# Decoder trunk: VectorE divides the fetched rows, the compressions begin ten k-tiles later with their loads ahead, stored gates get their Silus together, and the paired stages open with steps 0 0 1 1

## The chip, the cores and the metric

One core of a Trainium2 chip runs the kernel. The metric is the device time in microseconds (us). PE is the matmul engine, DVE is VectorE, ACT is ScalarE, POOL is GpSimd, and SP is the engine whose queue issues most DMAs.

## What is computed

One layer of a hybrid decoder: a normalised x (256 tokens, width 4096) goes through one input projection, the result feeds two attention mixers, each mixer's output is normalised and multiplied by a Silu gate, and both go through one output projection onto the residual.

```python
h = _rmsnorm(x, norm_g[l])
proj = h @ w_in[l]
(q_a, k_a, v_a, z_a, q_b, kc, vc, ksl, vsl, kwn, vwn, z_b, g_b) = jnp.split(proj, _split_points(), axis=-1)
o_a = _dilated_mixture(heads(q_a, N_HEADS_A) * (HEAD_DIM ** -0.5), heads(k_a, N_HEADS_A), heads(v_a, N_HEADS_A), slopes_a)
gates = jax.nn.sigmoid(g_b).reshape(B, S, N_HEADS_B, 3)
o_b = _nsa(heads(q_b, N_HEADS_B), kc, vc, ksl, vsl, kwn, vwn, gates, slopes_b, k_pe, k_w1, k_w2, v_pe, v_w1, v_w2)
y_a = _rmsnorm(o_a, out_g_a[l]) * jax.nn.silu(z_a)
y_b = _rmsnorm(o_b, out_g_b[l]) * jax.nn.silu(z_b)
x = x + jnp.concatenate([y_a, y_b], axis=-1) @ w_out[l]
return _rmsnorm(x, final_g)

def _compress(t, pe, w1, w2):       # of kc and of vc
    blocks = t[:, idx] + pe         # 15 blocks of 32 tokens
    return jax.nn.gelu(flat @ w1) @ w2
```

## The kernel before, in words

Every matrix product keeps float32 accuracy by splitting each operand into a high and a low part (`split_to`: ACT copies the high part at L105, DVE subtracts to get the low part at L106) and adding three matmuls (L98, L99, L100). So each block of weights is loaded on SP's queue, split on ACT and DVE, and then multiplied on PE.

The program has five parts. An **opening** (0 to 112 us of the trace) brings in x and computes the columns of kc, vc, kw and the small gates. The **paired input stage** (to about 847 us, `run_pairs`) takes nine pairs of 512-column chunks of w_in, 16 steps each; a fast step saves one of eight products by adding and subtracting blocks first (five DVE instructions, L432 to L439; 21 matmuls), a plain step splits the blocks as they are (one DVE instruction of L106; 24 matmuls). `FIRST` lists for the first pair of a stage which of its steps are fast (1) and plain (0). There are two places for split fast blocks (bf0, bf1) and one for plain blocks (bp). Results leave through POOL-issued DMAs that add into DRAM scratch (`put_sums`, L459). In this stage and its twin the order of the engines is the order of the code.

The **middle stage** (847 to about 1364 us) streams seven chunks of gate columns z (a1 to a3, b0 to b3; 32 k-tiles of six matmuls each) and the first chunk of w_out through PE. Between its k-tiles a list of tasks advances, one piece (up to a `yield`) for each unit of credit; a k-tile gives `pace` units. The tasks are two compressions (`compress`, of kc and of vc, four loads w1 of 1 MB each and 64 matmuls ph of 128x256), four dilated attentions (`attend_a`), `mixer_done` for mixer a, `start_b`, four sparse attentions (`attend_b`), `mixer_done` for b, and last `turn_y`. Here the framework's scheduler sets the order on each engine, and an engine keeps to its order: an instruction that waits holds all behind it. Rows of q, k, sel and qb in scratch were stored before the factor 1/rms (rstd) was put in, so `fetch(..., divide=True)` multiplies them on POOL as soon as they land (L560, two multiplies of 128x512 for each of 13 fetches); PE then transposes them (pt, L592). Values v are multiplied while they are split (L108, L109). `gate_z` takes Silu of each gate chunk as it is finished (L735); a chunk finished before its mixer goes to scratch and comes back later (L712, L720).

Work at the start of this stage: `begin_rest` issues the loads of the constants cmat and of kvc and puts all tasks on the list at once, so the first compression starts with the first k-tile, and its loads of pe, w2 and w1 are issued inside it, one by one.

The **paired output stage** (to about 1610 us) is the twin over w_out, three pairs; it begins with `first_chunk` (residual add, squares and a multiply on the w_out chunk just finished). A **last stage** of plain chunks and the final normalisation ends the program.

Of the kernel before, what the change touches and what calls it, by code (L numbers as in the profile page):

```python
# [11 lines left out]
F32 = mybir.dt.float32  # L12
# [6 lines left out]
P = 128  # L19
SEQ = 256  # L20
NT = SEQ // P
# [23 lines left out]
FIRST = [0, 0, 1, 0, 1, 1, 0, 1, 1, 0, 1, 1, 0, 1, 1, 0]  # L45
# [38 lines left out]
def hybrid_trunk(ctx: ExitStack, tc: tile.TileContext, a: dict):  # L84
# [310 lines left out]
    def run_pairs(w_src, dcs, lhs_of, sops, begin, places, names, out=False):  # L395
# [144 lines left out]

# [86 lines left out]
    def attend_a(hg):  # L627
        vsrc, qsrc = st.pop("va"), st.pop("qa")
        v = split_values(vsrc)
        ksrc = fetch(f"k{hg}", divide=True)  # L630
        yield
        yield from transposed(qsrc, "qa", SCALE)
        yield from transposed(ksrc, "ka")
        if hg < 3:
            st["va"], st["qa"] = fetch(f"v{hg + 1}"), fetch(f"q{hg + 1}", divide=True)
        else:
            st["sel"], st["kw"] = fetch("sel", divide=True), fetch("kw", 2 * HD)
# [66 lines left out]
    waiting, finished, gated = {"a": [], "b": []}, set(), set()  # L704

    def gate(which, i, sz=None):
        r = o_sb["r" + which]
        if sz is None:
            sz = []
            for m in range(NT):  # L710
                sz.append(room["zq"].tile([P, CW], F32, name="sz", tag="zt", bufs=4))
                nc.sync.dma_start(sz[m], scratch(f"z{which}{i}")[:, m])  # L712
            yield
            yield
            if (which, i) == ("a", 0):
                for m in range(NT):
                    nc.scalar.activation(sz[m], sz[m], AF.Silu, scale=rstd[:, m : m + 1])
        for m in range(NT):
            ys = o_at(which, i * CW, CW)[:, m]
            nc.vector.scalar_tensor_tensor(ys, ys, r[:, m : m + 1], sz[m], op0=OP.mult, op1=OP.mult)  # L720
        gated.add((which, i))
        yield

    def mixer_done(which):
        rms_of(which)
        finished.add(which)
        for i in waiting[which]:
            yield from gate(which, i)
        yield

    def gate_z(which, i):
        def done(ps):
            sz = [room["zq"].tile([P, CW], F32, name="sz", tag="zt", bufs=4) for m in range(NT)]
            for m in range(NT):
                nc.scalar.activation(sz[m], ps[m], AF.Silu, scale=rstd[:, m : m + 1])  # L735
            if which in finished:
                tasks.appendleft(gate(which, i, sz))
            else:
                for m in range(NT):
                    nc.sync.dma_start(scratch(f"z{which}{i}")[:, m], sz[m])  # L740
                waiting[which].append(i)
# [46 lines left out]

    def compress(t, which):

        n = "kv"[which]
# [7 lines left out]
        if which == 1:  # L799
            st["va"], st["qa"] = fetch("v0"), fetch("q0", divide=True)  # L800
        pe = room["work"].tile([P, CBL], F32, name="pe", tag="pe", bufs=2)
        nc.sync.dma_start(pe, a[f"cmp_{n}_pe"])
        w2 = room["zq"].tile([P, 2, HD], F32, name="w2", tag="zt", bufs=4)
        w2h = room["work"].tile([P, 2, HD], F32R, name="w2h", tag="pTh", bufs=2)
        w2l = room["work"].tile([P, 2, HD], F32R, name="w2l", tag="pTl", bufs=2)
        nc.sync.dma_start(w2, a[f"cmp_{n}_w2"])
        w1 = {}

        def load_w1(i):
            w1[i] = room["o"].tile([P, 2 * 4, HID], F32, name="w1", tag="o", bufs=4)  # L810
            nc.sync.dma_start(w1[i], a[f"cmp_{n}_w1"][i])

        yield
        bhl = room["o"].tile([P, CBL, 2, 2, NC], F32R, name="bhl", tag="o", bufs=4)
        load_w1(0)
# [9 lines left out]
        load_w1(1)  # L825
# [43 lines left out]
        if which == 0:  # L869
# [5 lines left out]
            nc.vector.memset(kc, 0.0)  # L875
# [19 lines left out]
    def start_b():  # L895
# [20 lines left out]
        put_k(1, kw)  # L916
        yield
# [5 lines left out]
        st["qb"] = fetch("qb0", divide=True)  # L923
# [7 lines left out]
    def attend_b(hg):  # L931
        yield from transposed(st.pop("qb"), "qb", SCALE)
        if hg < 3:
            st["qb"] = fetch(f"qb{hg + 1}", divide=True)
# [11 lines left out]
    def attend_half(hg, m):  # L946
# [36 lines left out]
        def compressed():  # L983
# [13 lines left out]
            nc.vector.memset(c3, 0.0)  # L997
# [101 lines left out]
    def first_chunk(ps, xr, gf):  # L1099

        for m in range(NT):
            r = xr[:, m]
            nc.vector.tensor_add(r, ps[m], r)
# [138 lines left out]
    def begin_rest():  # L1242
# [10 lines left out]
        t = fetch("kvc")  # L1253
# [49 lines left out]
    rest = run_pairs(a["w_out"], dcs, y_lhs, y_sops, begin_out, OUT_PLACES, OUT_BANKS, out=True)  # L1303
# [77 lines left out]
```

## Time and profile before

| | |
|---|---|
| time, median of 3 runs | 1671.77 us (1671.13 to 1672.93) |
| profiled execution, its own time | 1676.31 us |
| its span in the trace | 1674.4 us |
| PE busy | 1621.6 us, 97% of the span |
| DVE busy | 1375.1 us, 82% |
| ACT busy | 1011.5 us, 60% |
| POOL busy | 197.4 us, 12% |
| DMA | 386.71 MB, mean 231 GB/s |

The profiled execution took 4.54 us longer than the median of the runs; 1.91 us of its time lie outside the span. PE is busy nearly always, so what there is to win or lose in this change shows as PE's idle time and as stretches in which PE runs at a lower clock (PEclk: 1.00 is 2.4 GHz, 0.50 is 1.2 GHz).

### The profile page before, as it was taken

How to read it: one execution, taken by the hardware profiler on the slowest of the kernel's cores; microseconds unless marked ns; L12 is line 12 of the kernel's file. 1: busy time of each engine (PE TensorE's matmuls, PEld its weight loads, DVE VectorE, ACT ScalarE, POOL GpSimd, SP SyncE). 2: the span in 40 equal slices, each digit the busy share in tenths (PEclk: the TensorE clock that was granted, in tenths of full speed). 3: DMA queues.
4: the chain of work that ended last, by engine and by line, in shares of the span. 5: the costliest groups of instructions: out<-in, count | busy, mean ns of one | idle time of the engine just before them, and what ended most of it. 6: DMA issues, size and time to landing. Idle time of an engine off the chain costs nothing.

```text
span 1674.4 us, 20936 instructions
## 1 busy us (share of the span) xinstructions
PE 1621.6 (97%) x7743; PEld 1334.6 (80%) x7743; DVE 1375.1 (82%) x1651; ACT 1011.5 (60%) x1259; POOL 197.4 (12%) x224
## 2 busy tenths in 40 slices
PE   8999999999999999999989999899999999999997
PEld 5997778888878888888877777778888878778886
DVE  6769998898889898989857777787866859998984
ACT  6746656565656565656555656676665745656554
POOL 0000111020102020202022211200000000111110
PEclk9999999999999999999999999999999999999999
DMA  9766788887889797979797544443355456798974
GB/s 354 270 229 203 238 265 252 260 256 241 251 246 267 243 282 227 286 231 285 253 318 265 176 142 166 159 164 131 127 200 191 162 202 201 231 274 244 294 282 170
DMA packets 105286, 386.71 MB, mean 231 GB/s; under 512 B 12576, under 2 KB 13216, under 8 KB 93792
## 3 DMA queue, kind: packets, MB, share of 16 engines
q1 hardware_dynamic: 80928, 331.37, 56.3%
q0 software_dynamic: 23824, 52.97, 14.3%
q8 instruction: 60, 0.98, 0.2%
q10 hardware_dynamic: 432, 1.05, 0.2%
q14 instruction: 42, 0.34, 0.1%
HBM read 334.17 MB, written 53.26 MB: 231 GB/s over the span
## 4 chain that ended last, share of the span: by engine, by line
PE 74%; DVE 10%; DMA 6%; issue 5%; ACT 3%; POOL 1%; SPq 0%; ACTq 0%; POOLq 0%; DVEq 0%
PE p L99 14%; PE p L100 13%; PE p L98 13%; PE acc L99 8%; PE acc L100 7%; PE acc L98 7%; DMA bw<-in_w_in 3%; DVE bf L439 2%; PE e L100 2%; PE e L99 2%; PE e L98 2%; DVE bf L438 2%; DVE bt L432 1%; DVE wl L106 1%; DMA w<-in_cmp_v_w 1%
## 5 line engine op out<-in xcount | busy, mean ns | idle before, releaser
L106 DVE TENSOR_TENSOR wl<-w,wh 128x1024 fp32r<-128x1024 f32 (+2 forms) x178 | 209.0, 1176 | 111.1 <-ACT wh L105 110.5
L105 ACT ACTIVATE wh<-w 128x1024 fp32r<-128x1024 f32 (+2 forms) x178 | 180.6, 1018 | 128.4 <-PE acc L100 100.7
L98 PE MATMUL acc<-wh,xh 128*128 128x512 f32 (+2 forms) x640 | 243.3, 382 | 4.0 <-ACT wh L105 4.0
L99 PE MATMUL acc<-wl,xh 128*128 128x512 f32 (+2 forms) x640 | 242.7, 379 | 4.2 <-DVE wl L106 4.1
L439 DVE TENSOR_TENSOR bf<-bt,bf 128x2048 fp32r<-128x2048 f32 x108 | 246.7, 2284 | 0.0
L100 PE MATMUL acc<-wh,xl 128*128 128x512 f32 (+2 forms) x640 | 241.4, 377 | 0.0
L434 ACT ACTIVATE bf<-bt 128x1024 fp32r<-128x1024 f32 x108 | 114.5, 1060 | 187.1 <-DVE bt L432 186.9
L106 DVE TENSOR_TENSOR bp<-bw,bp 128x2048 fp32r<-128x2048 f32 x72 | 164.8, 2288 | 70.1 <-ACT bp L105 70.1
L431 ACT ACTIVATE bf<-bw 128x1536 fp32r<-128x1536 f32 x108 | 160.3, 1484 | 67.2 <-DMA bw<-in_w_in 45.5
L105 ACT ACTIVATE bp<-bw 128x2048 fp32r<-128x2048 f32 x72 | 137.5, 1910 | 88.4 <-PE e L100 69.7
L438 DVE TENSOR_TENSOR bf<-bw,bf 128x1536 fp32r<-128x1536 f32 x108 | 189.1, 1751 | 0.0
L432 DVE TENSOR_TENSOR bt<-bw 128x1024 f32<-128x1024 f32 x108 | 132.0, 1222 | 14.3 <-DMA bw<-in_w_in 11.8
L99 PEld LDWEIGHTS acc<-wl,xh 128*128 128x128 f32 x640 | 122.1, 191 | 23.9 <-DVE wl L106 7.2
L437 ACT ACTIVATE bf<-bt 128x1024 fp32r<-128x1024 f32 x108 | 114.8, 1063 | 42.9 <-DVE bt L436 41.8
L98 PEld LDWEIGHTS acc<-wh,xh 128*128 128x128 f32 x640 | 121.8, 191 | 22.8 <-ACT wh L105 5.5
L100 PEld LDWEIGHTS acc<-wh,xl 128*128 128x128 f32 x640 | 121.7, 190 | 18.7
L99 PE MATMUL p<-bf,sum 128*128 128x512 f32 x324 | 127.7, 394 | 5.3 <-DVE bf L439 5.2
L98 PE MATMUL p<-bf,sum 128*128 128x512 f32 x324 | 126.3, 390 | 0.0
L100 PE MATMUL p<-bf,sum 128*128 128x512 f32 x324 | 126.2, 390 | 0.0
L99 PE MATMUL p<-bp,xh 128*128 128x512 f32 x324 | 126.1, 389 | 0.0
L100 PE MATMUL p<-bp,xl 128*128 128x512 f32 x324 | 126.0, 389 | 0.0
L98 PE MATMUL p<-bp,xh 128*128 128x512 f32 x324 | 126.0, 389 | 0.0
(328 smaller groups left out, 3466.6 us busy)
## 6 DMA issues: line engine op xcount, KB each, us to landing
bw<-in_w_in SPq DMA_DIRECT2D x288, 512.0 KB, 6.3
w<-in_w_in SPq DMA_DIRECT2D x60, 1024.0 KB, 4.9
bw<-in_w_out SPq DMA_DIRECT2D x96, 512.0 KB, 5.0
w<-in_w_out SPq DMA_DIRECT2D x16, 1024.0 KB, 5.4
scr_q<-parts POOLq DMA_DIRECT2D x30, 256.0 KB, 7.9
scr_k<-parts POOLq DMA_DIRECT2D x30, 256.0 KB, 7.9
scr_v<-parts POOLq DMA_DIRECT2D x30, 256.0 KB, 7.8
scr_qb<-parts POOLq DMA_DIRECT2D x30, 256.0 KB, 8.3
```

Source lines behind the costliest of these rows:

```text
L98: nc.tensor.matmul(out, lh, rh, start=start, stop=False)
L99: nc.tensor.matmul(out, lh, rl, start=False, stop=False)
L100: nc.tensor.matmul(out, ll, rh, start=False, stop=stop)
L105: nc.scalar.activation(h, src, AF.Copy)
L106: nc.vector.tensor_sub(l, src, h.bitcast(F32))
L431: nc.scalar.activation(h[:, :3], w[:, B22:], AF.Copy)
L432: nc.vector.tensor_tensor(t[:, T3 : T1 + 1], w[:, B22 : B11 + 1], w[:, B12 : B12 + 1].to_broadcast([P, 2, CW]), op=OP.subtract)
L434: nc.scalar.activation(h[:, 3:5], t[:, T3 : T1 + 1], AF.Copy)
L437: nc.scalar.activation(h[:, 5:], t[:, T2:], AF.Copy)
L438: nc.vector.tensor_sub(l[:, :3], w[:, B22:], h[:, :3].bitcast(F32))
L439: nc.vector.tensor_sub(l[:, 3:], t, h[:, 3:].bitcast(F32))
```

## The change

Five edits go together.

1. `FIRST` is 0 0 1 1 0 1 1 ... in place of 0 0 1 0 1 1 0 ....
2. `fetch` only loads; a new `divide` multiplies by rstd on DVE, called where the rows are about to be transposed, some pieces of the task later. The zeroing of kc and of c3 moves from DVE to POOL.
3. The loads for the compressions are issued at k-tile 3 of the first z chunk (`load_first`) and the compressions start at k-tile 10 (`attentions`); w1 of both compressions is one row of eight loads that runs ahead. `pace` is 1.1 in the first z chunk and 1.5 later (1.45 before).
4. All gate chunks that finish before mixer b is done are stored without their Silu; `mixer_done` loads them two ahead and takes the Silus there. Chunks a3, b0 and b1, which were kept or gated at once before, go through scratch too.
5. In the output stage only the two residual adds stand ahead of the first step; the squares, the multiplies and the store of r0 come after its third step (`store_first`).

```diff
-FIRST = [0, 0, 1, 0, 1, 1, 0, 1, 1, 0, 1, 1, 0, 1, 1, 0]
+FIRST = [0, 0, 1, 1, 0, 1, 1, 0, 1, 1, 0, 1, 1, 0, 1, 0]
...
             split_on(n)
+            if n == 2 and later:
+                later()
...
-    def fetch(key, width=CW, divide=False):
+    def fetch(key, width=CW):
         t = room["zq"].tile([P, NT, width], F32, name="fetched", tag="qk", bufs=2)
         nc.sync.dma_start(t, scratch(key))
-        for m in range(NT if divide else 0):
-            nc.gpsimd.tensor_scalar_mul(t[:, m], t[:, m], rstd[:, m : m + 1])
         return t
+
+    def divide(t):
+
+        for m in range(NT):
+            nc.vector.tensor_scalar_mul(t[:, m], t[:, m], rstd[:, m : m + 1])
...
-        ksrc = fetch(f"k{hg}", divide=True)
+        ksrc = fetch(f"k{hg}")
+        yield
+        divide(qsrc)
         yield
         yield from transposed(qsrc, "qa", SCALE)
+        yield
+        divide(ksrc)
+        yield
         yield from transposed(ksrc, "ka")
...
     def mixer_done(which):
+
         rms_of(which)
         finished.add(which)
-        for i in waiting[which]:
-            yield from gate(which, i)
-        yield
+        loaded = deque()
+        todo = list(waiting)
+        waiting.clear()
...
+        load()
+        if todo:
+            load()
+        for _ in range(3):
+            yield
+        while loaded:
+            z, sz = loaded.popleft()
+            for m in range(NT):
+                nc.scalar.activation(sz[m], sz[m], AF.Silu, scale=rstd[:, m : m + 1] if z == ("a", 0) else 1.0)
+            yield
+            yield from gate(*z, sz)
+            if todo:
+                load()
+            yield
...
+            last = which in finished and "b" in finished
             for m in range(NT):
-                nc.scalar.activation(sz[m], ps[m], AF.Silu, scale=rstd[:, m : m + 1])
-            if which in finished:
+                nc.scalar.activation(sz[m], ps[m], AF.Silu if last else AF.Copy, scale=rstd[:, m : m + 1])
+            if last:
...
+    w1, small = {}, {}
+
+    def load_w1(i):
+
+        if i < 8:
+            w1[i] = room["o"].tile([P, 2 * 4, HID], F32, name="w1", tag="o", bufs=4)
+            nc.sync.dma_start(w1[i], a[f"cmp_{'kv'[i // 4]}_w1"][i % 4])
...
-                split_to(wh, wl, w1[grp // 2][:, hs])
+                split_to(wh, wl, w1[4 * which + grp // 2][:, hs])
                 ready[grp] = (wh, wl)
-                if grp % 2 == 1 and grp // 2 + 2 < 4:
-                    load_w1(grp // 2 + 2)
+                if grp % 2 == 1:
+                    load_w1(4 * which + grp // 2 + 2)
+                if grp == 4 and which == 0:
+                    load_small(1)
...
-            nc.vector.memset(kc, 0.0)
+            nc.gpsimd.memset(kc, 0.0)
...
+    def load_first():
+        st["kvc"] = fetch("kvc")
+        load_small(0)
+        load_w1(0)
+        load_w1(1)
...
-    pace = 1.45
-    waiting["a"].append(0)
+    hooks[0, 3] = load_first
+    hooks[0, 10] = attentions
...
-        add_chunk(w_chunk(c + i), CW, x_lhs, gate_z(which, i), pace=pace)
+        add_chunk(w_chunk(c + i), CW, x_lhs, gate_z(which, i), pace=1.5 if chunks else 1.1)
...
-        first_chunk(first_out, *room["in0"])
+        for m in range(NT):
+            r = room["in0"][0][:, m]
+            nc.vector.tensor_add(r, first_out[m], r)
...
+    def store_first():
+        first_chunk(*room["in0"])
```

SP's queue at the start of the middle stage, in the kernel before. Rows of L811 load w1 (cmp_k of the first compression, cmp_v of the second), L806 loads w2, L254 loads four k-tiles of the z chunk (1 MB; x3 is three such loads in a row), fetched is a fetch from scratch:

```order
L811 DMA w_5836<-in_cmp_k_w 128x2048
L254 DMA w<-in_w_in 128x2048
L806 DMA w_5825<-in_cmp_k_w 128x256
L811 DMA w_5855<-in_cmp_k_w 128x2048
L811 DMA w_5864<-in_cmp_k_w 128x2048
L811 DMA w_5906<-in_cmp_k_w 128x2048
L254 DMA w<-in_w_in 128x2048 x2
L558 DMA fetched<-scr_v_2627 128x1024
```

The same queue now, from behind the first two w1 loads (L820 is the load of w1 now):

```order
L820 DMA w_5842<-in_cmp_k_w 128x2048
L820 DMA w_5844<-in_cmp_k_w 128x2048
L254 DMA w<-in_w_in 128x2048 x3
L824 DMA pe<-in_cmp_v_pe 128x32
L560 DMA fetched<-scr_v_2627 128x1024
L826 DMA w_6011<-in_cmp_v_w 128x256
L254 DMA w<-in_w_in 128x2048
L820 DMA w_5950<-in_cmp_k_w 128x2048
L820 DMA w_5990<-in_cmp_k_w 128x2048
L820 DMA w_6036<-in_cmp_v_w 128x2048
L820 DMA w_6076<-in_cmp_v_w 128x2048
L254 DMA w<-in_w_in 128x2048 x3
```

The third w1 load (w_5950) stood behind one load of z; it stands behind four loads of z and the fetch of v0 now, and the first w1 loads of the second compression have moved up right behind the first compression's.

DVE at the end of the paired input stage and the first rows of the middle stage, before. bp and bf1 are the last split blocks of the paired stage, wl is the low part of two k-tiles of z, w1hl that of half a w1 load:

```order
L106 TENSOR_TENSOR bp_1153<-bw1_1151,bp_1153 128x2048
L106 TENSOR_TENSOR bf1_1154<-bw2_1152,bf1_1154 128x2048
L875 MEMSET kc_6050 128x32
L997 MEMSET c3_7889 128x384
L106 TENSOR_TENSOR wl_5758<-w_5755,wh_5757 128x1024
L106 TENSOR_TENSOR wl_5762<-w_5755,wh_5761 128x1024
L106 TENSOR_TENSOR wl_5768<-w_5765,wh_5767 128x1024
L820 TENSOR_TENSOR bt_5838<-cT_5816,pe_5823 128x480 x2
L106 TENSOR_TENSOR w1hl_5858<-w1_5836,w1hl_5858 128x1024
```

And now, from the last split of the paired stage on:

```order
L106 TENSOR_TENSOR bf1_1154<-bw2_1152,bf1_1154 128x2048
L106 TENSOR_TENSOR wl_5758<-w_5755,wh_5757 128x1024
L106 TENSOR_TENSOR wl_5762<-w_5755,wh_5761 128x1024
L106 TENSOR_TENSOR wl_5768<-w_5765,wh_5767 128x1024
L106 TENSOR_TENSOR w2l_5916<-w2_5840,w2h_5915 128x256
L106 TENSOR_TENSOR wl_5821<-w_5765,wh_5820 128x1024
L106 TENSOR_TENSOR w1hl_5932<-w1_5842,w1hl_5932 128x1024
L106 TENSOR_TENSOR w1hl_5947<-w1_5842,w1hl_5947 128x1024
L106 TENSOR_TENSOR wl_5849<-w_5771,wh_5848 128x1024
L106 TENSOR_TENSOR wl_5865<-w_5771,wh_5864 128x1024
```

The two MEMSETs no longer stand ahead of the first wl, and two splits of the first w1 load have come ahead of the splits of k-tiles 8 and 9 (wl_5849) and later ones.

DVE around the second attention's keys, now. va is the split of the values, qaTl and kaT are the low parts of turned queries and keys, o_a, den and n belong to the attention before:

```order
L669 RECIPROCAL rden_6710<-den_6703 128x2
L109 SCALAR_TENSOR_TENSOR va_6780<-fetched_6549,rstd_71,va_6780 128x4x128
L106 TENSOR_TENSOR wl_6807<-w_6737,wh_6806 128x1024
L106 TENSOR_TENSOR pal_6734<-pt_6729,pah_6733 128x384
L109 SCALAR_TENSOR_TENSOR qaTl_6796<-pt_6797,qaTh_6795 128x512
L109 SCALAR_TENSOR_TENSOR qaTl_6796<-pt_6816,qaTh_6795 128x512
L693 SCALAR_TENSOR_TENSOR o_a0_6553<-po_6755,rden_6710,o_a0_6553 128x128 x2
L566 TENSOR_SCALAR fetched_6785<-fetched_6785,rstd_71 128x512 x2
L106 TENSOR_TENSOR wl_6832<-w_6737,wh_6831 128x1024
L106 TENSOR_TENSOR kaT_6841<-pt_6842,kaT_6841 128x512
L106 TENSOR_TENSOR wl_6888<-w_6804,wh_6887 128x1024
```

The two divides (L566) stand in DVE's row ahead of the splits wl of the z chunk; before, they stood on POOL, with nothing of PE's stream behind them.

## Rows read from the trace of the kernel before

**Rows 1.** Stretches: length, busy PE, PEld, DVE, ACT, POOL; clock, DMA, GB/s.
```profile
840.00:860.00 20.00, 15.91 (x74) 12.63 (x73) 9.46 (x11) 7.93 (x12) 5.30 (x6) 1.00 0.94 297
860.00:890.00 30.00, 28.25 (x154) 22.46 (x151) 20.42 (x27) 16.50 (x22) 4.89 (x6) 1.00 1.06 349
890.00:1100.00 210.00, 190.94 (x989) 152.55 (x990) 159.56 (x380) 137.41 (x251) 43.67 (x25) 0.96 0.47 167
```

**Rows 2.** What PE waited for, 825 to 1370 us: total, times, longest.
```profile
PE pt L592 <- POOL fetched L560: 12.0, 8, 2.7
PE ph L842 <- DVE bhl L106: 5.6, 2, 3.0
PE acc L99 <- DVE wl L106: 2.9, 3, 1.5
PE pt L666 <- DVE n L656: 1.1, 5, 0.3
```

**Rows 3.** Stretches right after PE's waits (columns of rows 1).
```profile
892.30:895.70 3.40, 3.40 (x16) 3.40 (x17) 3.40 (x7) 0.00 (x0) 1.63 (x1) 0.50 1.01 424
...
953.70:957.10 3.40, 3.40 (x12) 2.82 (x10) 1.29 (x2) 2.15 (x5) 0.00 (x0) 0.50 0.51 159
...
1063.80:1069.00 5.20, 5.02 (x17) 4.45 (x18) 2.10 (x4) 1.62 (x3) 2.35 (x3) 0.50 0.51 179
```

**Rows 4.** The tile fetched: multiplies on POOL, ns min/median/max, first and last start.
```profile
L560 POOL TENSOR_SCALAR fetched<-fetched,rstd x26: 1557/1568/3647, 889.4 to 1117.2; 128x512 f32<-128x512 f32 x26
```

**Rows 5.** DVE groups of the last stage: a multiply of the same shape.
```profile
L1161 DVE TENSOR_SCALAR r<-r,rout 128x512 f32<-128x512 f32 x8 | 3.3, 481 | 1.4 <-POOL rout L115 1.4
```

**Rows 6.** The chain that ended last, DMAs in it: start, issue to landing.
```profile
868.46 16.73 DMA w<-in_cmp_v_w
...
945.20 3.75 DMA fetched<-scr_k
...
976.86 6.56 DMA fetched<-scr_k
```

**Rows 7.** SP's DMA queue, 840 to 905 us: packets, MB, share of 16 engines.
```profile
q1 hardware_dynamic: 3181, 17.46, 68.8%
```

**Rows 8.** Timeline, start of the middle stage: start, duration, instruction, idle before.
```profile
847.28 0.39 PE L98 MATMUL acc<-wh,xh 128*128 128x512 f32 x1
...
847.52 0.09 DVE L875 MEMSET kc<- 128x32 f32 x1 [9.23 <-PE e L100]
...
855.64 0.39 PE L98 MATMUL acc<-wh,xh 128*128 128x512 f32 x1
...
856.32 0.39 PE L98 MATMUL acc<-wh,xh 128*128 128x512 f32 x1
859.33 0.33 PE L842 MATMUL ph<-w1hl,bhl 128*60 128x256 f32 x1 [2.61 <-DVE bhl L106]
...
859.61 0.28 PE L842 MATMUL ph<-w1hl,bhl 128*60 128x256 f32 x1
859.72 0.28 PE L843 MATMUL ph<-w1hl,bhl 128*60 128x256 f32 x1
```

**Rows 9.** Timeline of ACT, 926 to 938 us: a Silu and a load of the function table.
```profile
929.53 0.69 ACT L735 ACTIVATE sz<-acc,rstd 128x512 f32<-128x512 f32 x1
930.24 1.28 ACT L655 ACT_TABLE_LOAD   x1
```

**Rows 10.** Timeline of DVE and PE, first pairs of the two paired stages.
```profile
137.48 0.50 PE L99 MATMUL p<-bf,sum 128*128 128x512 f32 x1 [1.24 <-DVE bf L439]
1372.55 1.22 DVE L432 TENSOR_TENSOR bt<-bw 128x1024 f32<-128x1024 f32 x1
1376.94 0.50 PE L99 MATMUL p<-bf,yh 128*128 128x512 f32 x1 [1.49 <-DVE bf L438]
1379.01 2.29 DVE L106 TENSOR_TENSOR bp<-bw,bp 128x2048 fp32r<-128x2048 f32 x1
1379.14 0.50 PE L99 MATMUL p<-bf,ysum 128*128 128x512 f32 x1 [1.24 <-DVE bf L439]
```

More of the change, by code (lines that the diff above doesn't have):

```diff
@@ L393, in hybrid_trunk, with run_pairs @@
     OUT_PLACES, OUT_BANKS = ("f1", "t", "p", "f0", "w"), ("p7", "p1", "p6", "p5", "p4", "p2", "p3", "e")
-    def run_pairs(w_src, dcs, lhs_of, sops, begin, places, names, out=False):
+    def run_pairs(w_src, dcs, lhs_of, sops, begin, places, names, out=False, later=None):
         fast, plain = [[i for i in range(NKP) if FAST[i] == f] for f in (1, 0)]
@@ L629, in attend_a @@
         v = split_values(vsrc)
-        ksrc = fetch(f"k{hg}", divide=True)
+        ksrc = fetch(f"k{hg}")
+        yield
+        divide(qsrc)
         yield
         yield from transposed(qsrc, "qa", SCALE)
+        yield
+        divide(ksrc)
+        yield
         yield from transposed(ksrc, "ka")
         if hg < 3:
-            st["va"], st["qa"] = fetch(f"v{hg + 1}"), fetch(f"q{hg + 1}", divide=True)
+            st["va"], st["qa"] = fetch(f"v{hg + 1}"), fetch(f"q{hg + 1}")
         else:
-            st["sel"], st["kw"] = fetch("sel", divide=True), fetch("kw", 2 * HD)
+            st["sel"], st["kw"] = fetch("sel"), fetch("kw", 2 * HD)
         qh, ql = st["qaT"]
@@ L702, in hybrid_trunk, with gate @@
     yh, yl, turned = [None] * 4, [None] * 4, set()
-    waiting, finished, gated = {"a": [], "b": []}, set(), set()
-    def gate(which, i, sz=None):
+    waiting, finished, gated = [("a", 0)], set(), set()
+    def gate(which, i, sz):
         r = o_sb["r" + which]
[L708 to L712, printed above, removed]
-            yield
[L714 to L717, printed above, removed]
         for m in range(NT):
@@ L726, in mixer_done, with load @@
         finished.add(which)
-        for i in waiting[which]:
-            yield from gate(which, i)
-        yield
+        loaded = deque()
+        todo = list(waiting)
+        waiting.clear()
+        def load():
+            z = todo.pop(0)
+            sz = [room["zq"].tile([P, CW], F32, name="sz", tag="zt", bufs=4) for m in range(NT)]
+            for m in range(NT):
+                nc.sync.dma_start(sz[m], scratch(f"z{z[0]}{z[1]}")[:, m])
+            loaded.append((z, sz))
+        load()
[12 more added lines that the diff above has]
+            yield
     def gate_z(which, i):
@@ L740, in done @@
                     nc.sync.dma_start(scratch(f"z{which}{i}")[:, m], sz[m])
-                waiting[which].append(i)
+                waiting.append((which, i))
         return done
@@ L787, in open_b, with load_small @@
         B["vc3"] = room["work"].tile([3 * Q, 2, HD], F32R, name="vc3", bufs=1)
+    w1, small = {}, {}
[3 more added lines that the diff above has]
+            nc.sync.dma_start(w1[i], a[f"cmp_{'kv'[i // 4]}_w1"][i % 4])
+    def load_small(which):
+        pe = room["work"].tile([P, CBL], F32, name="pe", tag="pe", bufs=2)
+        nc.sync.dma_start(pe, a[f"cmp_{'kv'[which]}_pe"])
+        w2 = room["zq"].tile([P, 2, HD], F32, name="w2", tag="zt", bufs=4)
+        nc.sync.dma_start(w2, a[f"cmp_{'kv'[which]}_w2"])
+        small[which] = pe, w2
     def compress(t, which):
-        n = "kv"[which]
         tT = room["zq"].tile([P, 2, NT, P], F32, name="cT", tag="zt", bufs=4)
@@ L799, in compress @@
         if which == 1:
[L800 to L803, printed above, removed]
+            st["va"], st["qa"] = fetch("v0"), fetch("q0")
+        pe, w2 = small.pop(which)
         w2h = room["work"].tile([P, 2, HD], F32R, name="w2h", tag="pTh", bufs=2)
         w2l = room["work"].tile([P, 2, HD], F32R, name="w2l", tag="pTl", bufs=2)
[L806 to L811, printed above, removed]
         yield
         bhl = room["o"].tile([P, CBL, 2, 2, NC], F32R, name="bhl", tag="o", bufs=4)
-        load_w1(0)
         bt = room["work"].tile([P, CBL, 2, NC], F32, name="bt", tag="qTh", bufs=1)
@@ L824, in compress @@
         yield
-        load_w1(1)
         ph = room["pso"].tile([4 * NC, HID], F32, name="ph", tag="po")
@@ L916, in start_b @@
         put_k(1, kw)
+        divide(sel)
         yield
@@ L922, in start_b @@
         yield
-        st["qb"] = fetch("qb0", divide=True)
+        st["qb"] = fetch("qb0")
         put_v(1, vg[:, :, : 2 * HD])
@@ L931, in attend_b @@
     def attend_b(hg):
-        yield from transposed(st.pop("qb"), "qb", SCALE)
+        for _ in range(0 if hg else 3):
+            yield
+        qb = st.pop("qb")
+        divide(qb)
+        yield
+        yield from transposed(qb, "qb", SCALE)
         if hg < 3:
-            st["qb"] = fetch(f"qb{hg + 1}", divide=True)
+            st["qb"] = fetch(f"qb{hg + 1}")
         first, second = attend_half(hg, 0), attend_half(hg, 1)
@@ L996, in compressed @@
             c3 = live["c"] = room["work"].tile([P, 4, 3, Q], F32, name="c3", tag="c3", bufs=1)
-            nc.vector.memset(c3, 0.0)
+            nc.gpsimd.memset(c3, 0.0)
             for i in range(3):
@@ L1295, in begin_out @@
     def begin_out():
-        first_chunk(first_out, *room["in0"])
+        for m in range(NT):
+            r = room["in0"][0][:, m]
+            nc.vector.tensor_add(r, first_out[m], r)
         psum.close()
         room["banks"] = opened(psum, "banks", 1, space=PS)
+    def store_first():
+        first_chunk(*room["in0"])
         right2.close()
@@ L1302, in hybrid_trunk @@
     ordered.enter_context(tc.manual_schedule())
-    rest = run_pairs(a["w_out"], dcs, y_lhs, y_sops, begin_out, OUT_PLACES, OUT_BANKS, out=True)
+    rest = run_pairs(a["w_out"], dcs, y_lhs, y_sops, begin_out, OUT_PLACES, OUT_BANKS, out=True, later=store_first)
     inner.close()
```

6 lines of the change are left out of this document (3 added, 3 removed).

## The prediction

> **What bounds the kernel now.** PE is busy 97% of the span, so I looked for the stretches where it is not, by stage first. In the middle stage PE loses 4.1 us from 840 to 860, 1.8 us to 890 and 19.1 us to 1100 [rows 1]; and from 890 to 1100 its mean clock is 0.96. Next, the waits of PE in that stage: 12.0 us in eight waits for POOL's multiply of fetched rows, 5.6 us for bhl (the low part of a compression's blocks), 2.9 us for wl; waits that go back to ACT are small [rows 2]. Then what follows a wait. After three of the long idle times PE ran on at a granted clock of 0.50, the 1.2 GHz level: 3.4 us at 892.3, 3.4 us at 953.7 (again at 1015.2), and 5.2 us at 1063.8 [rows 3]. Work done at half the clock costs half the stretch: 1.7, 1.7, 1.7 and 2.6 us. So a wait of about 3 us costs nearer 5 us. The rest of the program shows little: a wait of 1.24 us in the first pair of the input stage, and 1.49 and 1.24 us in the first pair of the output stage [rows 10].
>
> **The multiplies on POOL.** One of them took 1.56 us at least and 3.65 us at most [rows 4], two per fetch, started when the rows land. On DVE the nearest row, same shape and type, is 0.48 us [rows 5]. What goes: 12.0 us of waits and the three stretches behind them, 1.7 + 1.7 + 2.6 = 6.0 us, **18.0** in all. What comes: 26 x 0.48 = 12.5 us more on DVE, of which 24 fall where the attentions are; DVE's 159.6 us of 210 become 172, which is still not a bound. But a divide can't run before its rows land, and now it stands in DVE's order ahead of splits wl that PE's stream needs. The fetch of keys was 3.75 us long in one case and 6.56 us in another [rows 6]. The code puts five pieces of a task between the fetch of keys and its divide; at 1.5 pieces a k-tile that is 3.3 k-tiles. Three matmuls take 0.68 us [rows 8], a k-tile of six 1.36 us, so the cover is 4.5 us: enough for the short landing, 2.0 us too little for the long one. Seven divides stand close behind a fetch or a transfer that had no cover (q0, the four keys, sel, qb0). The best case is 0; the worst, 7 x 2.0 us and three stretches at half clock, is 19. I take a third of the long case each time, 7 x 0.7 = 4.9, and one stretch of 1.7: **-6.6**. It is nearer the low end because splits of z run up to two blocks (four k-tiles) ahead of PE, so a DVE wait of 1 or 2 us need not reach PE.
>
> **The second compression.** Its wait for bhl (3.0 us, the longer of two) and the 1.7 us at 892.3 came while the DMA engines were full (share 1.06 to 890). It now starts some 14 k-tiles later, with its pe, w2 and the first two w1 ahead. I leave 0.7 us of it: **+4.0** (0 to 4.7).
>
> **The first compression.** Two waits go. The first wl stood behind the two MEMSETs, which wait 9.2 us for the paired stage's last matmuls [rows 8]; now it waits for nothing late (up to 1.5 us, [rows 2]). The wait before 859.33 (2.6 us, with bhl and w1 just landed) loses its cause, since kvc and two w1 are issued ahead. With the small ones for w1hl that was about 4.9 us. Against this stands SP's queue: the third w1 load is behind eight items. Up to its end the queue must carry cmat 0.8, kvc 0.5, w2 0.1, two w1, three loads of z, v0 0.5, w2 0.1, another z and itself, together 9.0 times 1.05 MB. From 840 to 905, with the DMA engines full, SP's loads got 17.46 MB in 65 us [rows 7], 3.9 us for one load; the POOL-issued adds took much of the rest. So it lands near 842 + 35.3 = 877.3. It is needed by PE at k-tile 17: 847.28 + 17 x 1.36 + 0.6 for the transposes + 32 matmuls ph at 0.117 [rows 8] = 874.7, and 2.1 us earlier for its two splits: 872.6. PE waits 4.7 us, and I add one stretch of half clock, 1.7: 6.4 against 4.9, **-1.5**. Two splits of the first w1 now ahead of wl of k-tiles 8 and 9 may take 1 to 2 us of this wait earlier, which moves it but doesn't add. Bounds: no wait if the queue gets the 349 GB/s of 860 to 890 [rows 1] for itself (9.0 loads in 27 us, landing at 869), so +4.9. At worst it takes the 16.73 us of the slowest w1 [rows 6], issued when k-tile 14 frees its buffer at 847.28 + 14 x 1.36 = 866.3: it lands at 883.0, 10.4 us late, 12.1 with the clock, so -7.2.
>
> **The function table.** Counted in the instruction order, there are 18 loads before and 4 after; 14 x 1.28 [rows 9] = 18 us of ACT time. ACT is busy 137 of 210 us, so only what sits in an attention's chain counts. The largest wait of PE that goes back to ACT's exponentials is that for n, 1.1 us [rows 2]. I take **+1.0** (0 to 1.1). The ten Silus more on ACT and four more transfers of stored gates have the idle DMA share of 0.47 to hide in; without it they would cost a load's delay, not PE time. The table load at 930.24 [rows 9] starts where the Silu ends (929.53 + 0.69 = 930.22), with nothing between. The Trainium skill (ScalarE: Activation LUTs, What ACT_TABLE_LOAD costs) puts a drain on top of the load, about 2.7 us in all. This trace shows the load's 1.28 and no drain beside it. By the page the 14 would be 37 us of ACT, the term 2.0 instead of 1.0, and the sum 1 us better.
>
> **The paired stages.** In the input stage the second fast step moves up one place, so its DVE split follows the first without waiting for the plain place, and the 1.24 us at 137.48 should go: **+1.2** (0 to 1.2; the price, if the shift opens a new wait, is one of the same size, -1.2). In the output stage, 2.7 us of waits come from the first fast split, which starts at 1372.55 behind the two squares and multiplies. Without them it starts 3 us earlier and both waits end. But the second fast step now comes straight behind the first. Its split lasts 1372.55 to 1379.01, 6.5 us on DVE, while PE needs 21 x 0.227 = 4.8 us for the first: 1.7 us of new wait, and the moved squares come in front of a later split. **0** (-1.5 to +2.7).
>
> **The sum.** 18.0 - 6.6 + 4.0 - 1.5 + 1.0 + 1.2 + 0 = 16.1 us. It is made against the profiled execution, 1676.31 to 1660.2. That execution lies 4.5 us above the median of the runs, so I take the difference from the median: 1671.77 - 16.1 = **1655.7 us**.
>
> **Rivals.** *All of it:* the divides never wait (+6.6) and the third w1 is in time (+6.4): 16.1 + 13.0 = 29, less 1 for bhl, gives 1644. For it: a split order two blocks ahead, and five pieces of cover. Against it: the full queue up to 890. *The compression's wait stays and grows:* the third w1 at its worst, 12.1 in place of 6.4, gives 10.4 us, 1661. *The landings eat half:* waits of 1.5 us at seven divides and two more stretches at half clock, 13.9 instead of 6.6, gives 8.8 us, 1663. *Slower:* one mechanism, the in-order divide of the four keys and three other fetches on DVE. Each one that waits holds wl, exponent sums and transposes together, where POOL held only the transposes. It turns the sign when the seven waits with their clock cost 6.6 + 16.1 = 22.7 us, 3.2 us each, that is landings of 7.7 us against 4.5 of cover. The longest landing in the two rows is 6.56; if the stored gates' transfers and z loads coincide with every fetch and add 2 us, it would be 8.5 us each, 4.0 of wait, 28 us, and the time 1677. Three gate transfers more in this stage speak for it, a DMA share of 0.47 against it. *The gains are not there:* if PE's eight waits pass to the landing itself, since POOL started as the rows came, then only the multiply's own length (3.1 less 1.0 us, at eight waits counted by half, 8 us) goes and the rest balances: 1664.
>
> **How the numbers follow.** A measurement of this kernel can tell about 0.2%, 3.3 us, from no change. Main case (1650 to 1660) 0.47; all of it 0.17; larger w1 wait 0.10; landings eat half or the multiply alone 0.17, of which a third ends within 0.2%; slower 0.06, and 0.03 that unknown waits just cancel the gains. So faster 0.85, within 0.2% 0.09, slower 0.06. The range that leaves out 2 in 10 goes from 1643 (all of it, with the output stage's 2.7) to 1667 (landings, less the input stage's 1.2 and the function table).
>
> **What would show it.** Right: no wait of pt on POOL; divides of about 0.5 us on DVE; clock 1.00 through 940 to 1070; the table loads 4; no idle at the first wl; a wait of ph on w1 near 872 to 877; the wait at 137 gone. Wrong: idle DVE ahead of L566 with DMA as its releaser and PE waiting on wl behind it, more stretches at 0.50, or a wait of the z stream for its own loads (bigger queue) near k-tile 28.

## The result and the profile after

The changed kernel takes 1653.95 us (median of 4 runs, 1652.93 to 1655.78), the kernel before 1672.35 us in the same session: 18.4 us less, ratio 0.9888 with a 95% interval of 0.9871 to 0.9906. The prediction was 1655.7, a gain of 16.1 us. The size is right, but two of its terms are not, and they are off in opposite directions; the experiments below show by how much.

The stretches of the middle stage in the trace of the changed kernel (columns of [rows 1]):

```profile
840.00:860.00 20.00, 18.70 (x82) 14.66 (x81) 7.32 (x7) 8.69 (x12) 4.56 (x7) 1.00 1.06 326
860.00:890.00 30.00, 22.70 (x113) 18.46 (x112) 16.61 (x16) 12.80 (x14) 2.86 (x4) 0.83 0.98 331
890.00:1100.00 210.00, 206.83 (x1105) 166.07 (x1104) 176.59 (x419) 138.03 (x260) 1.83 (x3) 1.00 0.55 193
...
875.80:886.00 10.20, 6.55 (x23) 5.57 (x24) 5.37 (x5) 5.09 (x6) 0.00 (x0) 0.50 0.82 310
```

Against [rows 1], PE's idle time from 890 to 1100 has fallen from 19.1 to 3.2 us, and its clock there is 1.00. From 860 to 890 it is the other way: 7.3 us idle where there were 1.8, and 10.2 us at half clock where there were none. DVE went from 159.6 to 176.6 us between 890 and 1100 and is still not full.

What PE waited for from 825 to 1360 us (total, times, longest), to be read beside [rows 2]:

```profile
PE ph L872 <- ACT w1hl L105: 5.8, 1, 5.8
PE acc L99 <- DVE wl L106: 1.5, 3, 1.1
PE p L99 <- DVE bf L439: 1.2, 1, 1.2
PE ph L873 <- DVE w1hl L106: 0.8, 1, 0.8
PE pt L676 <- DVE n L666: 0.7, 3, 0.3
PE ph L872 <- DVE bhl L106: 0.7, 1, 0.7
PE pt L597 <- issue: 0.6, 1, 0.6
PE po L688 <- ACT pah L105: 0.4, 1, 0.4
PE pv L98 <- ACT rh L105: 0.3, 1, 0.3
PE pt L597 <- DVE fetched L566: 0.3, 1, 0.3
```

The 12.0 us of waits for the multiply on POOL have become 0.3 us for the divide on DVE. In their place at the top stands one wait of 5.8 us, of the first compression for its third w1. More views of the changed kernel show both ends. The first fence has the group of the divides on DVE between 840 and 1340 (count, busy and mean ns, idle time ahead and what ended it) and the wait in DVE's list that belongs to them. The second has three pieces of the chain that ended last: the split of an earlier load of z, the issue of the next load of z on SP's queue, and the load of the third w1 (start, issue to landing). Behind them stand the first matmul of z and the first matmul that needed this w1, from PE's timeline:

```profile
L566 DVE TENSOR_SCALAR fetched<-fetched,rstd 128x512 f32<-128x512 f32 x26 | 11.8, 479 | 1.5 <-DMA fetched<-scr_k 1.4
...
DVE fetched L566 <- DMA fetched<-scr_k: 1.4, 1, 1.4
```

```profile
860.10 1.23 DVE wl L106
861.35 0.33 SPq L254
861.73 15.72 DMA w<-in_cmp_k_w
...
842.01 0.39 PE L98 MATMUL acc<-wh,xh 128*128 128x512 f32 x1
...
878.66 0.47 PE L872 MATMUL ph<-w1hl,bhl 128*60 128x256 f32 x1 [5.79 <-ACT w1hl L105]
```

A divide lasts 0.479 us, as its nearest row of before said (0.481). In all 26 of them DVE stood idle for a landing only 1.5 us, nearly all of it once. The w1 landed at 877.45 us (861.73 + 15.72).

### The profile page after: what moved, and what is told of

The parts are those of the page before. It is cut to its first block, busy times and chain, and to the rows that moved or that the text cites. A ratio compares the mean times of both kernels' runs of the same rounds, so it can differ in the third digit from the quotient of the medians.

```text
span 1651.8 us, 20933 instructions
## 1 busy us (share of the span) xinstructions
PE 1615.9 (98%) x7743; PEld 1330.4 (81%) x7743; DVE 1377.4 (83%) x1668; ACT 999.4 (61%) x1255; POOL 153.6 (9%) x207
## 3 DMA queue, kind: packets, MB, share of 16 engines
q10 hardware_dynamic: 432, 1.05, 0.2%
## 4 chain that ended last, share of the span: by engine, by line
PE 81%; DVE 8%; DMA 5%; issue 3%; ACT 3%; SPq 0%; ACTq 0%; POOLq 0%; POOL 0%; DVEq 0%
PE p L99 15%; PE p L100 15%; PE p L98 15%; PE acc L99 8%; PE acc L100 8%; PE acc L98 8%; DMA w<-in_w_in 2%; PE e L100 2%; PE e L99 2%; PE e L98 2%; DVE bf L439 2%; DVE bt L432 1%; DVE bf L438 1%; DMA w<-in_cmp_k_w 1%; PE pt L1051 1%
```

## Experiments

Each ratio is that of the kernel's runs to runs of the kernel before on the same chip, with its 95% interval. Differences between two variants are given as differences of their medians, though they ran on different chips; taken from the ratios they come out up to 1.8 us otherwise.

**1. The engine alone, in the kernel before.**

```diff
-            nc.gpsimd.tensor_scalar_mul(t[:, m], t[:, m], rstd[:, m : m + 1])
+            nc.vector.tensor_scalar_mul(t[:, m], t[:, m], rstd[:, m : m + 1])
```

> The kernel before with one edit: the 26 multiplies by rstd run on VectorE instead of GpSimd, at the same place in the code (right behind the fetch). If the length of GpSimd's multiply (two of 1.56 us and more) was the price, the eight waits of 12.0 us shrink to about half and two or three stretches at half clock go: 1660 to 1665 us. If instead the later place of the divide in the changed kernel is what counts, little changes: 1669 to 1673. If VectorE, waiting in order for landings, holds the splits of the z stream, it is slower than before: over 1675.

Measured: 1653.7 us against 1673.65, ratio 0.9882 (0.9867 to 0.9898). One word gives the whole of the changed kernel's gain. The stretches in its trace:

```profile
840.00:860.00 20.00, 15.82 (x73) 12.53 (x72) 11.53 (x13) 8.20 (x11) 5.11 (x6) 0.95 1.00 316
860.00:890.00 30.00, 28.07 (x148) 22.71 (x146) 20.57 (x28) 17.91 (x23) 4.32 (x5) 0.98 1.06 354
890.00:1100.00 210.00, 205.44 (x1109) 165.82 (x1110) 180.99 (x455) 149.07 (x282) 0.72 (x1) 1.00 0.52 184
```

The compressions, untouched, lose what they lost before (840 to 890: 6.1 us idle against 5.8). From 890 to 1100 idle time falls by 14.5 us. The stretches at half clock there go as well: 1.7, 1.7, 1.7 and 2.6 us of [rows 3], but one of the same length is new before 890, at the first compression's wait (0.05 x 20 + 0.02 x 30 = 1.6 us by the clocks of these rows). Together 14.5 + 7.7 - 1.6 - 0.3 = 20.3, against the 20.0 us that were measured between the medians. (The two profiled executions lie further apart, 1674.4 against 1650.1 us.) The idea that only the later place of the divide counts falls with this run, and so does the slower rival: with the divide right behind the fetch in the code, DVE stood idle for a landing 1.0 us in all, and PE waited 0.2 us for a divide.

**2. The changed kernel with the multiply back on GpSimd**, right behind the fetch; `divide` does nothing and all new pieces of the tasks stay.

```diff
+        for m in range(NT if divided else 0):
+            nc.gpsimd.tensor_scalar_mul(t[:, m], t[:, m], rstd[:, m : m + 1])
         return t
...
-        for m in range(NT):
-            nc.vector.tensor_scalar_mul(t[:, m], t[:, m], rstd[:, m : m + 1])
+        return
```

> The changed kernel with one edit undone: the multiplies run on GpSimd right behind each fetch, but all new pieces of the tasks between fetch and transposes stay. If the engine is what counts, TensorE waits for GpSimd's multiply again, 6 to 12 us with the clock: 1660 to 1667 us. If the added pieces (about two k-tiles, 2.7 us, more between a fetch and its transposes) already hide GpSimd's multiply, it is within 0.2% of the changed kernel: 1651 to 1657.

Measured: 1673.47 us against 1673.65, ratio 0.9999 (0.999 to 1.0009): all of the gain is gone, more than I expected. Its waits of PE, and the multiply on POOL (ns min/median/max):

```profile
PE pt L598 <- POOL fetched L562: 10.7, 7, 4.0
PE ph L873 <- ACT w1hl L105: 4.9, 1, 4.9
...
L562 POOL TENSOR_SCALAR fetched<-fetched,rstd x26: 1559/1580/3625, 903.5 to 1134.4; 128x512 f32<-128x512 f32 x26
...
1080.29 0.48 PE L598 MATMUL pt<-ident,fetched 128*128 128x128 f32 x1 [4.04 <-POOL fetched L562]
```

The waits are back, 10.7 us in seven, in spite of two more k-tiles between fetch and transposes. The clock from 920 to 1100 is 0.95 again. With both this wait and that for w1 in it, the kernel is as slow as before.

**3. Three loads of w1 ahead instead of two.**

```diff
         load_w1(1)
+        load_w1(2)
...
-                    load_w1(4 * which + grp // 2 + 2)
+                    load_w1(4 * which + grp // 2 + 3)
```

> The changed kernel with three loads of w1 issued at k-tile 3 instead of two, and each later one issued a load earlier, so the third stands ahead of all z loads of that stretch. If the 5.8 us wait for the third w1 and the 10 us of half clock behind it are one cost of the queue's order, both go: 8 to 12 us faster than the changed kernel, 1642 to 1646 us. If the full queue only hands the lateness on to the z loads of k-tiles 12 to 20, TensorE waits for wl there instead: 1650 to 1656.

Measured: 1651.31 us, ratio 0.9868 (0.9852 to 0.9883); the interval overlaps the changed kernel's. The wait for w1 is gone from PE's list, and waits of the z stream have come:

```profile
PE acc L99 <- DVE wl L106: 3.4, 4, 1.1
PE acc L98 <- ACT wh L105: 1.7, 1, 1.7
```

From 840 to 890 PE is idle 4.5 us, where the changed kernel has 8.6. So about half of the lateness was handed on to the z stream, as the second theory had it, and the time lies in that theory's range: w1's place in the queue is only part of what is short.

**4. Start at k-tile 14.**

```diff
-    hooks[0, 10] = attentions
+    hooks[0, 14] = attentions
```

> The changed kernel with the compressions starting at k-tile 14 instead of 10. If the third w1 is late against a fixed queue, 5.4 us more of cover shorten its wait to 0 to 3 us (one more z load comes ahead of it, 3.9 us) and the half clock behind it may go: 1645 to 1651 us. If the later start only moves the same wait, within 0.2% of the changed kernel: 1651 to 1657.

Measured: 1649.39 us, ratio 0.9856 (0.9839 to 0.9873). It is inside the first theory's range, though its interval just overlaps that of the changed kernel. The wait for w1 went from 5.8 to 4.5 us only. The third w1 stands behind one more load of z: it was issued 24.2 us after the first matmul of z, in the changed kernel 19.7.

```profile
PE ph L872 <- ACT w1hl L105: 4.5, 1, 4.5
```

**5. Start at k-tile 24, loads from k-tile 12.**

```diff
-    hooks[0, 3] = load_first
-    hooks[0, 10] = attentions
+    hooks[0, 12] = load_first
+    hooks[0, 24] = attentions
```

> The changed kernel with the first loads issued at k-tile 12 instead of 3 and the compressions starting at k-tile 24 instead of 10. If the first compression's cost (in the changed kernel 5.8 us of wait for the third w1, about 4 us of smaller waits from 850 to 880, and 10.2 us at half clock, 5.1 lost) comes from loading 4 MB of w1 while the paired stage's adds still hold the DMA engines, it goes: 8 to 14 us faster than the changed kernel, 1640 to 1646 us. If the loads are merely late wherever they are put, or the attentions pushed back meet the next stage, 1650 or more.

Measured: 1646.29 us, ratio 0.9836 (0.9822 to 0.9851), 7.7 us under the changed kernel; 0.3 us outside the range expected. The stretches:

```profile
840.00:860.00 20.00, 18.83 (x81) 14.72 (x80) 7.22 (x7) 9.28 (x12) 3.82 (x5) 1.00 1.04 338
860.00:890.00 30.00, 30.00 (x146) 24.64 (x145) 17.78 (x16) 13.54 (x14) 4.43 (x7) 1.00 1.05 358
```

The DMA engines are as full as before (1.04, 1.05), but the compression's first matmul ph now comes at 885.03 (865.48 in the changed kernel), near the end of that stretch, and PE loses 1.2 us instead of 8.6, all at full clock. Two things were moved at once, the loads and the start; which of them does it is not separated.

**6. Edit 3 undone**: compressions at the first k-tile, their loads inside them, pace 1.45.

```diff
-    hooks[0, 3] = load_first
-    hooks[0, 10] = attentions
+    pace = 1.45
...
-        add_chunk(w_chunk(c + i), CW, x_lhs, gate_z(which, i), pace=1.5 if chunks else 1.1)
+        add_chunk(w_chunk(c + i), CW, x_lhs, gate_z(which, i), pace=pace)
```

> The changed kernel with edit 3 undone: compressions from the first k-tile, their loads issued inside them, pace 1.45; edits 1, 2, 4 and 5 stay. By the prediction's terms edit 3 is worth +4.0 - 1.5 = 2.5 us, so this would be 1656 us. By the traces of the changed kernel and of the first experiment, edit 3 loses about 7 us from 840 to 890 and gains 3 at the second compression: 1648 to 1651.

Measured: 1648.73 us, ratio 0.9854 (0.9839 to 0.9869), 5.2 us faster than with edit 3. The expectation from the traces is confirmed, the prediction's terms are not. The stretch from 920 to 1100, this kernel first and then the changed one:

```profile
920.00:1100.00 180.00, 178.56 (x943) 145.48 (x942) 147.87 (x364) 118.99 (x231) 1.57 (x3) 1.00 0.53 188
```

```profile
920.00:1100.00 180.00, 176.83 (x938) 141.26 (x937) 151.38 (x383) 117.15 (x233) 1.83 (x3) 1.00 0.54 187
```

In these two executions 1.7 us of the difference lie here in the attentions. From the first matmul of z to the first of the output stage the difference is 6.6 us (below).

**7. Edit 4 undone**: `gate`, `mixer_done` and `gate_z` as before.

```diff
-                nc.scalar.activation(sz[m], ps[m], AF.Silu if last else AF.Copy, scale=rstd[:, m : m + 1])
-            if last:
+                nc.scalar.activation(sz[m], ps[m], AF.Silu, scale=rstd[:, m : m + 1])
+            if which in finished:
```

> The changed kernel with edit 4 undone: Silu where a gate chunk is finished, a3, b0 and b1 not stored, 18 loads of the function table again. By the prediction's term of 1.0 us: 1655 us, not told from 1654. If the loads of the table lie in the attentions' chain once nothing else holds them, 2 to 5 us slower, 1656 to 1659.

Measured: 1654.63 us, ratio 0.9889 (0.9872 to 0.9906), the same as the changed kernel. Its trace has 16 loads of the function table, the changed kernel's 4. They are worth nothing that can be measured here.

**8. Edit 1 undone** in both paired stages.

```diff
-FIRST = [0, 0, 1, 1, 0, 1, 1, 0, 1, 1, 0, 1, 1, 0, 1, 0]
+FIRST = [0, 0, 1, 0, 1, 1, 0, 1, 1, 0, 1, 1, 0, 1, 1, 0]
```

> The changed kernel with edit 1 undone: steps 0 0 1 0 1 1 in both paired stages. By the prediction's terms 1.2 us slower in the input stage (the wait at 137 is back) and the output stage the same: 1655 us, seen only in the traces' windows. If the wait of 1.03 us at 194 belongs to the new order it goes, and the input stage comes out within 0.4 us; in the output stage the two waits of the first pair (1.40 and 1.05) go, up to 2.5 us faster: 1652.

Measured: 1654.35 us, ratio 0.9889 (0.9875 to 0.9904): the same. The time can't tell. The traces can, and show why: the list gains in one stage what it loses in the other. From the input stage's first matmul to the first issue of its first pair's results (L457) it is 80.9 us in all three traces with the old list (before, 1 and this one) and 79.7 to 79.8 in the eleven with the new. From the output stage's first matmul to the start of its last it is 250.6 us here, as in experiments 11 and 12, which also have the old list there, and 251.7 to 252.7 in the nine traces with the new. PE's waits in the input stage and in the first pair of the output stage, beside [rows 10]:

```profile
195.64 0.50 PE L99 MATMUL p<-bp,xh 128*128 128x512 f32 x1 [0.87 <-DVE bp L106]
...
1359.61 0.50 PE L99 MATMUL p<-bf,ysum 128*128 128x512 f32 x1 [1.23 <-DVE bf L439]
1375.93 0.50 PE L99 MATMUL p<-bf,ysum 128*128 128x512 f32 x1 [0.88 <-DVE bf L439]
```

The wait at 137 is gone and one of 0.87 us has come at 195, in the second pair; in the output stage two waits of 1.49 and 1.24 us are two of 1.23 and 0.88, and yet that stage is longer; where it loses is open.

**9. Each divide twice.**

```diff
             nc.vector.tensor_scalar_mul(t[:, m], t[:, m], rstd[:, m : m + 1])
+            nc.vector.tensor_scalar_mul(t[:, m], t[:, m], ones[:, 0:1])
```

> The changed kernel with every divide followed by a second multiply of the same shape, by ones: 26 more instructions of 0.48 us on VectorE, 12.5 us. If the divides cost nothing because VectorE has room where they stand, it stays within 0.2% of the changed kernel: 1651 to 1657 us. If each lies in the attentions' chain or ahead of splits that TensorE needs, some of the 12.5 us shows, 1658 to 1666.

Measured: 1658.57 us, ratio 0.9921 (0.9906 to 0.9937), 4.6 us slower than the changed kernel; the two intervals touch. The added group:

```profile
L567 DVE TENSOR_SCALAR fetched<-fetched,ones 128x512 f32<-128x512 f32 x26 | 12.5, 498 | 0.1
```

12.5 us more on DVE show as about 4.6 us of time (5.5 by the ratios). In the traces the middle stage, from the first matmul of z to the first of the output stage, is 2.7 us longer, 501.8 against 499.1, with PE's clock at half for 6.8 us in place of 10.2. So the divides seem not to be free: by this, something like a third of their 11.8 us may be paid.

**10. Edit 5 undone**: squares, multiplies and the store ahead of the output stage's first step.

```diff
-    def store_first():
         first_chunk(*room["in0"])
...
-    rest = run_pairs(a["w_out"], dcs, y_lhs, y_sops, begin_out, OUT_PLACES, OUT_BANKS, out=True, later=store_first)
+    rest = run_pairs(a["w_out"], dcs, y_lhs, y_sops, begin_out, OUT_PLACES, OUT_BANKS, out=True)
```

> The changed kernel with edit 5 undone: the squares, multiplies and the store of r0 stand ahead of the output stage's first step again. The prediction gave edits 1 and 5 together 0 in this stage. If the 3 us of VectorE work hold up the first fast split, its two waits (1.65 and 1.40 us in the kernel before) come back in some form, up to 3 us slower: 1654 to 1657, in the trace a longer wait between 1350 and 1360. If they only move a wait that the second fast split has anyway, no difference in time.

Measured: 1655.17 us, ratio 0.9906 (0.9889 to 0.9922). The intervals overlap; 1.2 us in the medians (3.0 by the ratios) is less than can be told.

**11. Start at k-tile 24, and the old list of first steps in the output stage only.**

```diff
+FIRST_OUT = [0, 0, 1, 0, 1, 1, 0, 1, 1, 0, 1, 1, 0, 1, 1, 0]
...
-        first = [(fast if f else plain).pop(0) for f in FIRST]
+        first = [(fast if f else plain).pop(0) for f in (FIRST_OUT if out else FIRST)]
...
-    hooks[0, 3] = load_first
-    hooks[0, 10] = attentions
+    hooks[0, 12] = load_first
+    hooks[0, 24] = attentions
```

> The start at k-tile 24 (loads from k-tile 12) and, in the output stage alone, the old list of first steps. The start takes away the first compression's waits, as measured at 1646.3 us; the output stage's list by the traces' windows is worth about 1.3 us (7.6 us of lost TensorE time from 1340 to 1480 in the changed kernel, 6.3 with the old list). If both add: 1643 to 1646 us. If the second is only another place of the same wait: 1645 to 1648.

Measured: 1641.34 us, ratio 0.9817 (0.9801 to 0.9833), faster than both theories gave. The intervals of this run and of experiment 5 still overlap. The output stage itself is 1.2 us shorter (250.6 against 251.8 us from its first to its last matmul), as the windows had said. Part of the 5.0 us (3.2 by the ratios) can't be the edit's. The opening (0 to 112 us, columns of [rows 1]), which the edit doesn't touch, in experiment 5 and then here:

```profile
0.00:112.00 112.00, 105.97 (x601) 90.94 (x602) 74.85 (x128) 74.94 (x119) 3.75 (x9) 0.98 0.79 292
```

```profile
0.00:112.00 112.00, 106.85 (x610) 91.40 (x611) 76.43 (x131) 75.64 (x120) 3.76 (x9) 1.00 0.80 298
```

0.9 us less idle, and no stretch at half clock.

**12. The same with a pace of 1.45.**

```diff
-pace=1.5 if chunks else 1.1)
+pace=1.45 if chunks else 1.1)
```

> The kernel of the eleventh experiment (start at k-tile 24, old list of first steps in the output stage) with a pace of 1.45 instead of 1.5 after the first z chunk. Undoing edit 3 left TensorE 1.4 us of idle time from 920 to 1100, where the changed kernel has 3.2; one difference between them is the pace. If the pace is the reason, the idle time falls by 1 to 2 us and the time to 1638 to 1641 us. If it is the places where tasks and k-tiles happen to meet, no difference that can be told from 1641.3, and waits at other places.

Measured: 1640.36 us, ratio 0.981 (0.9795 to 0.9825): not told apart from experiment 11 in time, but PE's idle time from 920 to 1100 falls from 3.9 us there to 1.5 us:

```profile
920.00:1100.00 180.00, 178.47 (x942) 144.37 (x941) 148.06 (x349) 117.64 (x222) 1.14 (x2) 1.00 0.56 194
```

The time speaks neither for nor against the pace. The idle time speaks for it between these two, but not as a rule: in the same window it is 1.8 us in experiment 4 and 1.7 in experiment 7, both with 1.5, and 3.4 in experiment 1 with 1.45. The place where tasks and k-tiles happen to meet is not excluded. This is the fastest version here, 13 us under the changed kernel and 32 under the one before.

## Why the prediction was right, and where its terms were not

**The multiplies on POOL.** The mechanism was right, and the term was too small: 18.0 - 6.6 = 11.4 predicted, 20.0 measured by experiment 1. The mis-sized part is "a third of the long case each time", the 6.6 us for divides that wait in order. DVE stood idle for a landing 1.5 us in all (1.0 in experiment 1), PE waited 0.3 us, and no stretch at half clock followed: the landings were nearly always in time, and whether splits two blocks ahead would have covered a longer one is not shown. The waits and the clock behind them came whole. The stretch at 892.3, which I had put down to the second compression, is gone in experiment 1, though that compression's wait is still there; but one of the same length stands at 857.9, behind the first compression's wait, so nothing is won by it. Why the clock fell at one of these waits and not at the other is open. Against the gain, experiment 9 points to a cost that I had set to nothing: DVE's own time in the attentions, about a third of it. It is within the 20.0, which are net.

That the engine counts, and not the place of the multiply in the code, is shown twice, by 1 (engine alone: all of the gain) and 2 (engine back: none of it). That GpSimd's multiply cost its time by slowing VectorE, and not by its own length, is a rival to which the traces leave little room: the splits wl took 1243 ns in the mean between 890 and 1100 before, 1219 in experiment 1, which for the 43 of them is 1.0 us. Not shown is why its multiply took 1.56 us in one case and 3.6 in another. The Trainium skill (SBUF — State Buffer, Who interferes with whom) says that GpSimd and VectorE share a pair of ports, and that a VectorE instruction with two SBUF inputs contends with a GpSimd one that reads SBUF. The spread of [rows 4] and of experiment 2 (1559 to 3625 ns) agrees with it in kind; no run here isolates it.

**The compressions.** The step that failed is "-1.5" with "+4.0", together +2.5: experiment 6 gives -5.2. The second compression's wait did go. But three things were wrong. First, the landing: it was foreseen at 877.3 and measured at 877.45, and that is luck. I had counted 35.3 us for the queue from 842.0, where its first load (cmat) was issued in the trace of before. In the changed kernel that load was issued at 836.8, and the same loads took 40.7 us. The paired stage ended 5.3 us earlier in this trace (first matmul of z at 842.01, against 847.28), the queue took 5.4 us more, and the two cancelled. The chain shows what the sum of loads left out: the load of z ahead of the third w1 was issued only when a split wl had ended (860.10 + 1.23), so this w1 could not be issued before 861.73. Counted from the first matmul of z, it landed after 35.4 us instead of 30.0 and its first split took 1.2 us instead of 2.1; PE came for it after 30.9 us (878.66 - 5.79 - 842.01) instead of 27.4, and so it waited 5.8 us and not 4.7. The earlier end of the paired stage is not the reason: in experiment 8 the first matmul of z came at 847.01, and the same wait is 5.9 us. Second, the small waits that I said would merge into it (wl, bhl and w1hl) stayed beside it: PE was idle 8.6 us from 840 to 890. Third, the stretch at half clock lasted 10.2 us, not 3.4. Its first 2.9 us fell into the wait itself; PE was busy 6.6 us of it, 3.3 lost. Experiments 3 to 5 say what the bound is: another order of the queue takes away about half of the idle time (3), a start four k-tiles later shortens the wait by 1.3 us (4), and a start near the end of the stretch in which the DMA engines are full takes it away (5).

**The function table**, +1.0: nothing that can be told (7).

**The paired stages**, +1.2 and 0: the wait named went, and by the traces the first pair of the input stage is 1.2 us shorter, as the term said. In the output stage the new list costs about as much (experiments 8 and 11), inside the bounds of -1.5 to +2.7. Edit 5 alone can't be told from nothing (10).

**The sum.** 20.0 for the engine and -5.2 for edit 3 leave 14.8 of the 18.4 us; the rest is edits 1, 4 and 5 and the few microseconds by which these programs differ from run to run. The two errors, +8.6 and -7.7, nearly cancelled: that the time came out within 2 us is in part luck. Of the rivals, the slower one is refuted by 1, and so is the one without the gains, since PE waited 0.3 us for the divides; the first half of "all of it" came true; the larger wait for w1 came about in half.

The middle stage alone, in the traces, says the same. Here are its end in the kernel before (first matmul of the output stage; its first matmul of z is in [rows 8]), its start and end in experiment 1, its end in the changed kernel, and its start and end in experiment 6:

```profile
1364.19 0.39 PE L98 MATMUL p<-bf,yh 128*128 128x512 f32 x1
...
845.12 0.39 PE L98 MATMUL acc<-wh,xh 128*128 128x512 f32 x1
1339.65 0.39 PE L98 MATMUL p<-bf,yh 128*128 128x512 f32 x1
...
1341.11 0.39 PE L98 MATMUL p<-bf,yh 128*128 128x512 f32 x1
...
844.43 0.39 PE L98 MATMUL acc<-wh,xh 128*128 128x512 f32 x1
1336.96 0.39 PE L98 MATMUL p<-bf,yh 128*128 128x512 f32 x1
```

That is 516.9 us before, 494.5 with the engine alone, 499.1 in the changed kernel and 492.5 with edit 3 undone: 22.4 for the engine, -6.6 for edit 3, and 2.0 for the rest of the change.

## What to carry to other kernels

An engine that is 12% busy can still be the one that PE waits for: look at the length of its single instruction between a landing and the first use, and try the same operation on another engine before any reordering. Where a stage begins while the last one's DMAs still fill the queue, putting loads ahead moves much of the wait instead of ending it; put the need for them near the end of that stretch. A wait of some microseconds on PE should be priced with the clock behind it, and an operation on a fuller engine that seems hidden should be tested by doing it twice.

## What the runs showed of the hardware

In the changed kernel the granted clock fell 2.9 us into the wait of 5.8 us and was 0.50 for 10.2 us; in experiments 7, 8 and 9 the same wait (5.9, 5.9 and 6.2 us) brought 6.8 us at 0.50. In the kernel before it was 3.4 to 6.8 us at waits of about 3 (the stretch of 5.2 in [rows 3] is part of one from 1063.0 to 1069.8) and none after the wait of 2.6 us that ended at 859.33 [rows 8], where the clock stays at 1.00 [rows 1]. The same multiply of fetched rows, 128x512, took 0.479 us on VectorE, every time between 466 and 487 ns, and on GpSimd between 1557 and 3647 ns [rows 4]:

```profile
L566 DVE TENSOR_SCALAR fetched<-fetched,rstd x26: 466/478/487, 904.2 to 1133.9; 128x512 f32<-128x512 f32 x26
```

Two programs that differ in nothing up to 112 us differed there by 0.9 us of idle time and by a stretch at half clock (experiments 5 and 11), which is as large as most of the single edits here. With one and the same input stage, eleven executions (one for each variant that has the new list) reached the first matmul of z between 840.8 and 845.5 us.
